# GpSimd subtracts half of the low parts for the first group of a DeltaNet layer

## The chip, the cores and the metric

The kernel runs on one core of a Trainium2 chip. A core has five engines with queues of their own: TensorE (PE in the rows; PEld is its weight load), VectorE (DVE), ScalarE (ACT), GpSimd (POOL) and SyncE (SP), which here issues the DMAs. The metric is the device time of one execution in microseconds; lower is better.

## The reference, cut to what matters

Two decoder layers on 512 tokens of width 1024 in float32. The first layer mixes tokens with a gated DeltaNet (8 heads of 128) beside 4 memory cross-attention heads; the second uses forgetting attention. The part that matters is the DeltaNet's input side:

```python
proj = h @ w_in
qkv = silu(causal_depthwise_conv(proj[..., :3 * MIX_WIDTH], conv_w))
z = proj[..., 3 * MIX_WIDTH: 4 * MIX_WIDTH]
q = l2_norm(split_heads(qkv[..., :MIX_WIDTH])) * HEAD_DIM ** -0.5
k = l2_norm(split_heads(qkv[..., MIX_WIDTH: 2 * MIX_WIDTH]))
v = split_heads(qkv[..., 2 * MIX_WIDTH:])
...
t_mat = triangular_solve(eye + a_mat, eye)      # per head and chunk
...
o = rms_norm(o, o_norm_w) * silu(split_heads(z))
```

## The kernel before, in words

Every projection is a product of float32 matrices, done in three matmuls (`mm3`, lines 157 to 159): each operand is split into a high part, which is a rounded copy, and a low part, which is the operand less that copy. For weights the split is made in `prepare`. Weights come in slabs of 128 partitions by 2048 columns, in two halves of 1024. For each half ScalarE makes the high part (L298) and then one engine subtracts (L299):

```python
for i in range(2):
    hi = self.wh.tile([P, 1024], F32R, ...)
    lo = self.wl.tile([P, 1024], F32R, ...)
    eng = nc.gpsimd if i and self.help else nc.vector
    ...
        nc.scalar.activation(hi[:, c], raw[i][:, c], AF.Copy)
        eng.tensor_sub(lo[:, c], raw[i][:, c], hi[:, c].bitcast(F32))
```

So with `self.help` set, the second half of a slab is subtracted by GpSimd, otherwise both halves by VectorE. In the kernel before, the flag is set for a while in the opening stage (the memory's keys and values) and is off from there on.

`slab` hands out the next slab that is ready and then calls `prepare(1)`, so that the slab after it is split while the present one is multiplied. The pools hold three raw tiles (`wr`), four high and four low halves, that is, two slabs. `fetch` issues the raw loads from SyncE; the order of all slabs is one list (`plan_weights`).

In `layer0_mixer` the keys come first, in four slabs of 256 columns (`gemm_feat`). Then the heads are done in two groups of four (`for g in range(2)`): two slabs of values, two of queries, both by `gemm_feat` with a convolution (`conv`: L727 on ScalarE, three steps L730 on VectorE that read PSUM, SiLU L732), and two of the gate z (`gemm_tok`, L1057). A slab is 48 matmuls of 512 columns.

Between these matmuls other work is interleaved. It is written as generators, which `pump` advances by a planned time after each `mm3`, so the order on TensorE is settled when the program is built; the order on the other engines follows from the dependences and a scheduler, and each engine runs its own queue in order. In the stretch of group 0 the interleaved work is: `dn_A` and `dn_inverse` of the DeltaNet (31 steps of two VectorE instructions each, L807 and L809, both inputs in SBUF; then two transposes L812, L813), and the four memory heads (`mem_heads`, `mem_attn`): cutting the queries (L451, L452), scores, maximum L639, exponential L642, reciprocal L643, normalization on GpSimd L644, transposes on TensorE, split L654 and L655. `group_scale` before them uses GpSimd at L429 and L435; the rsqrt by Newton steps is L207 to L211 on VectorE.

Of the kernel before, what the change touches and what calls it, by code (L numbers as in the profile page):

```python
# [41 lines left out]
class Kern:  # L42
# [962 lines left out]
    def layer0_mixer(self, hT):  # L1005
        nc, a = self.nc, self.a
        ab = self.const([P, NT, 16], "ab")
        qraw = self.slot(HD)
        qv = qraw.rearrange("p (t h) d -> p t (h d)", t=NT)

        def e0(t, ps):
            nc.scalar.copy(ab[:, t, :], ps[:, 0:16])
            nc.scalar.copy(qv[:, t, 0:256], ps[:, 16:272])

        def e1(t, ps):
            nc.scalar.copy(qv[:, t, 256:512], ps)

        self.gemm_tok(hT, e0, N=272, by_tile=True, need=lambda t: f"hx{t}")
        self.A = [self.slot(P) for _ in range(2)]
        self.spawn("dn", self.dn_gates(ab))  # L1020
        self.spawn("dn", self.dn_decays())
        self.gemm_tok(hT, e1, N=256)
        self.drain("rm")
        self.kT = [self.slot(T) for _ in range(2)]
        self.Ac = self.slot(1024)

        def ek(h, ps):
            self.conv(8 + h, ps, self.kT[h // 4][:, h % 4])
            self.spawn(f"dn{h % 2}", self.dn_A(h))

        for s in range(4):
            self.gemm_feat(hT, ek, 2 * s)
        self.spawn("mem", self.mem_heads(0, qraw))
        left = list(range(H))

        def merges():
            while "inverse" not in self.marks:
                yield 0.0
            while left:
                h = left.pop(0)  # L1040
                yield from self.dn_merge(h)
                self.free += 3
                self.marks.add(f"inv{h}")

        self.spawn("dn", self.dn_inverse())
        for i in range(3):
            self.spawn(f"dn{i}", merges())
        self.v, self.qT, self.z, self.mix = [None] * 2, [None] * 2, [None] * 2, [None] * 2
        for g in range(2):
            def ev(h, ps):  # L1050
                self.spawn("v", self.dn_v(h, self.conv(16 + h, ps)))

            def eq(h, ps):
                self.conv(h, ps, self.qT[g][:, h % 4])

            def ez(t, ps):
                nc.scalar.activation(self.z[g][:, t, :], ps, AF.Silu)  # L1057

            self.v[g] = self.slot(P)
            for s in range(2):  # L1060
                self.gemm_feat(hT, ev, 4 * g + 2 * s)
            self.qT[g] = self.slot(T)
            for s in range(2):
                self.gemm_feat(hT, eq, 4 * g + 2 * s)
            self.z[g] = self.slot(512)
            self.gemm_tok(hT, ez)
            self.drain("v")
            self.spawn("rec", self.dn_group(g))
# [463 lines left out]
```

## Time and profile before

| | us |
|---|---|
| median of 3 runs (lowest, highest) | 1437.98 (1436.66, 1438.18) |
| profiled execution, its own time | 1438.26 |
| its span, first to last instruction | 1436.6 |
| TensorE busy in the span | 1408.9 |
| VectorE busy in the span | 979.1 |
| ScalarE busy in the span | 688.4 |
| GpSimd busy in the span | 237.8 |

The times are of whole executions; the span leaves out what lies around the first and last instruction. Busy times are sums over the whole span; a stage can look quite different from the mean.

### The profile page before, as it was taken

The numbers are of one execution on the slowest core, as the hardware profiler recorded it, in microseconds if no ns is written. First come the engines' busy times: TensorE is split into PE (matmuls) and PEld (weight loads), VectorE is DVE, ScalarE is ACT, GpSimd is POOL, SyncE is SP. The second block draws the span as 40 slices with busy tenths as digits, with TensorE's granted clock in tenths as the row PEclk, the third lists the DMA queues.
The fourth block names the chain that finished last, engine by engine and source line by source line (L and its number), as shares of the span: only waits on it lengthen the run. The fifth ranks groups of instructions, "written<-read, shape, count | busy, mean of one in ns | idle before, by whom it ended". The sixth has DMA issues, their size and how long they took to land.

```text
span 1436.6 us, 19839 instructions
## 1 busy us (share of the span) xinstructions
PE 1408.9 (98%) x7442; PEld 1184.2 (82%) x7442; DVE 979.1 (68%) x1857; ACT 688.4 (48%) x1209; POOL 237.8 (17%) x321
## 2 busy tenths in 40 slices
PE   8999999989999999999999999999899999999999
PEld 6988777878889888888889888888788888888887
DVE  6679988477675677587657655665767567768663
ACT  6554764655344545444324454554534454554430
POOL 2274323222000000000001433533320000000000
PEclk9999999999999999999999999999999999999999
DMA  7542232134243151321226222224224315142122
GB/s 255 168 154 74 66 103 68 60 89 147 60 176 112 51 176 59 117 88 60 80 84 203 87 92 89 81 89 169 66 95 147 113 36 183 50 143 80 42 88 73
DMA packets 49634, 149.84 MB, mean 104 GB/s; under 512 B 5570, under 2 KB 10242, under 8 KB 49284
## 3 DMA queue, kind: packets, MB, share of 16 engines
q1 hardware_dynamic: 49392, 148.54, 31.6%
q8 instruction: 58, 0.95, 0.3%
q14 instruction: 36, 0.29, 0.1%
q10 hardware_dynamic: 148, 0.06, 0.0%
HBM read 141.20 MB, written 7.37 MB: 103 GB/s over the span
## 4 chain that ended last, share of the span: by engine, by line
PE 84%; DVE 10%; ACT 2%; issue 2%; DMA 1%; POOL 1%; SPq 0%; POOLq 0%; ACTq 0%; DVEq 0%
PE acc L157 20%; PE acc L158 19%; PE acc L159 19%; PE aux L159 6%; PE aux L157 6%; PE aux L158 6%; PE aux L164 3%; PE aux L169 3%; DVE wl L299 2%; DVE cv L730 1%; DVE slot L809 1%; DVE slot L807 1%; DVE cv L411 1%; DVE slot L1264 1%; ACT wh L298 0%
## 5 line engine op out<-in xcount | busy, mean ns | idle before, releaser
L157 PE MATMUL acc<-slot,wh 128*128 128x512 f32 (+1 forms) x832 | 314.3, 378 | 0.0
L299 DVE TENSOR_TENSOR wl<-wr,wh 128x1024 fp32r<-128x1024 f32 (+3 forms) x192 | 231.7, 1211 | 120.6 <-ACT wh L298 110.8
L158 PE MATMUL acc<-slot,wh 128*128 128x512 f32 (+1 forms) x832 | 310.9, 374 | 0.1
L159 PE MATMUL acc<-slot,wl 128*128 128x512 f32 (+1 forms) x832 | 310.8, 374 | 0.0
L298 ACT ACTIVATE wh<-wr 128x1024 fp32r<-128x1024 f32 (+3 forms) x194 | 197.0, 1016 | 199.4 <-PE acc L159 95.8
L157 PE MATMUL acc<-wh,slot 128*128 128x512 f32 (+3 forms) x740 | 285.0, 385 | 6.2 <-ACT wh L298 6.2
L158 PE MATMUL acc<-wl,slot 128*128 128x512 f32 (+3 forms) x740 | 276.8, 374 | 0.0
L159 PE MATMUL acc<-wh,slot 128*128 128x512 f32 (+3 forms) x740 | 276.3, 374 | 0.0
L159 PEld LDWEIGHTS acc<-slot,wl 128*128 128x128 f32 x832 | 156.7, 188 | 27.7
L157 PEld LDWEIGHTS acc<-slot,wh 128*128 128x128 f32 x832 | 156.7, 188 | 26.4
L158 PEld LDWEIGHTS acc<-slot,wh 128*128 128x128 f32 x832 | 156.9, 189 | 26.0 <-DVE slot L420 0.3
L157 PEld LDWEIGHTS acc<-wh,slot 128*128 128x128 f32 x740 | 140.7, 190 | 27.7 <-ACT wh L298 6.2
L1296 DVE TENSOR_TENSOR wl<-slot,wh 128x1024 fp32r<-128x1024 f32 x84 | 101.3, 1222 | 89.8 <-ACT wh L1295 89.8
L159 PEld LDWEIGHTS acc<-wh,slot 128*128 128x128 f32 x740 | 140.1, 189 | 24.7 <-DVE slot L1166 0.2
L158 PEld LDWEIGHTS acc<-wl,slot 128*128 128x128 f32 x740 | 140.7, 190 | 20.3 <-DVE wl L299 0.4
L1295 ACT CAST wh<-slot 128x1024 fp32r<-128x1024 f32 x84 | 88.3, 1052 | 92.8 <-PE acc L158 46.3
L157 PE MATMUL aux<-wh,t 128*128 128x512 f32 x336 | 130.8, 389 | 0.0
L159 PE MATMUL aux<-wh,t 128*128 128x512 f32 x336 | 130.7, 389 | 0.0
L158 PE MATMUL aux<-wl,t 128*128 128x512 f32 x336 | 130.7, 389 | 0.0
L429 POOL TENSOR_TENSOR cv<-slot 128x512 f32<-128x512 f32 x26 | 31.3, 1217 | 463.9 <-ACT slot L1189 421.0
L1264 DVE TENSOR_TENSOR slot<-slot,acc 128x512 f32<-128x512 f32 (+1 forms) x81 | 54.7, 677 | 51.4 <-PE acc L159 51.3
L1384 ACT ACTIVATE cv<-acc 128x512 f32<-128x512 f32 x64 | 37.6, 594 | 107.0 <-PE acc L159 107.0
(262 smaller groups left out, 1944.0 us busy)
## 6 DMA issues: line engine op xcount, KB each, us to landing
wr<-in_w_mlp SPq DMA_DIRECT2D x80, 512.0 KB, 4.3
slot<-in_w_mlp SPq DMA_DIRECT2D x48, 512.0 KB, 8.0
wr<-in_w_out SPq DMA_DIRECT2D x24, 512.0 KB, 3.8
wr<-in_fox_kq SPq DMA_DIRECT2D x16, 512.0 KB, 3.8
slot<-in_x SPq DMA_DIRECT2D x8, 512.0 KB, 6.6
wr<-in_dn_k SPq DMA_DIRECT2D x8, 512.0 KB, 4.3
wr<-in_dn_v SPq DMA_DIRECT2D x8, 512.0 KB, 3.7
wr<-in_dn_q SPq DMA_DIRECT2D x8, 512.0 KB, 3.8
```

Of the source, the lines that this page charges most:

```text
L157: mm(out, l[0], r[0], start=start, stop=False, **kw)
L158: mm(out, l[0], r[1], start=False, stop=False, **kw)
L159: mm(out, l[1], r[0], start=False, stop=stop, **kw)
L164: self.nc.tensor.matmul(out, l, r, start=start, stop=stop)
L169: self.nc.tensor.transpose(out, in_, self.ident)
L298: nc.scalar.activation(hi[:, c], raw[i][:, c], AF.Copy)
L299: eng.tensor_sub(lo[:, c], raw[i][:, c], hi[:, c].bitcast(F32))
L429: nc.gpsimd.tensor_mul(sq, raw[:, i:i + 4, :], raw[:, i:i + 4, :])
L1264: self.nc.vector.tensor_add(xv, xv, ps)
L1295: nc.scalar.copy(hi, r)
L1296: nc.vector.tensor_sub(lo, r, hi.bitcast(F32))
L1384: nc.scalar.activation(r, ps, AF.Relu)
```

## The change

One line sets the flag at the start of each group: on for group 0, off for group 1. `prepare` then gives the subtraction of each slab's second half to GpSimd for the slabs that are split while the flag is on.

```diff
@@ -1056,6 +1056,7 @@
             def ez(t, ps):
                 nc.scalar.activation(self.z[g][:, t, :], ps, AF.Silu)
 
+            self.help = g == 0
             self.v[g] = self.slot(P)
             for s in range(2):
                 self.gemm_feat(hT, ev, 4 * g + 2 * s)
```

## Rows read from the trace of the kernel before

**Rows 1.** The page: busy us of an engine, share of the span, instructions.

```profile
PE 1408.9 (98%) x7442; PEld 1184.2 (82%) x7442; DVE 979.1 (68%) x1857; ACT 688.4 (48%) x1209; POOL 237.8 (17%) x321
```

**Rows 2.** Busy times by window: stretch, length, busy us (instructions) by engine.

```profile
core 0: us, PE busy (x) PEld busy (x) DVE busy (x) ACT busy (x) POOL busy (x), PEclk, DMA share, GB/s
...
140.00:207.00 67.00, 61.87 (x304) 49.06 (x302) 65.40 (x124) 45.96 (x83) 17.47 (x18) 1.00 0.30 91
207.00:260.00 53.00, 50.15 (x561) 39.11 (x562) 36.20 (x69) 28.43 (x60) 22.65 (x29) 1.00 0.23 71
```

**Rows 3.** The chain of waits from 110 to 215 us: start, us, what.

```profile
164.25 4.03 DVE cv L730 x6
...
174.49 1.11 POOL t L644
...
207.07 0.54 DVE t L452
```

**Rows 4.** TensorE's waits, 140 to 220 us: total us, times, longest.

```profile
PE aux L169 <- POOL t L644: 3.6, 5, 1.7
```

**Rows 5.** Line 299: VectorE's from 118 to 197 us, GpSimd's in the whole kernel.

```profile
L299 DVE TENSOR_TENSOR wl<-wr,wh x11: 1209/1215/1757, 118.3 to 195.8; 128x1024 fp32r<-128x1024 f32 x11
...
L299 POOL TENSOR_TENSOR wl<-wr,wh x2: 2356/2378/2401, 15.9 to 22.6; 128x1024 fp32r<-128x1024 f32 x2
```

**Rows 6.** Timeline of GpSimd and VectorE in the opening stage.

```profile
22.62 2.40 POOL L299 TENSOR_TENSOR wl<-wr,wh 128x1024 fp32r<-128x1024 f32 x1 [4.37 <-ACT wh L298]
...
22.73 2.31 DVE L211 SCALAR_TENSOR_TENSOR sm<-sm,sm 128x2 f32<-128x2 f32 x1
```

**Rows 7.** Timeline of GpSimd and VectorE at 118 and at 173 us.

```profile
118.51 1.89 POOL L429 TENSOR_TENSOR cv<-slot 128x512 f32<-128x512 f32 x1 [3.14 <-ACT slot L732]
...
119.42 0.74 DVE L730 SCALAR_TENSOR_TENSOR cv<-acc,par,cv 128x509 f32<-128x509 f32 x1
...
172.85 1.11 POOL L644 TENSOR_TENSOR t<-t,sm 128x512 f32<-128x512 f32 x1 [4.88 <-DVE sm L643]
...
173.09 1.14 DVE L809 TENSOR_TENSOR slot<-slot 128x252 f32<-128x252 f32 x1
```

**Rows 8.** Timeline: six casts, the VectorE instructions behind them, L644, the first gate matmul.

```profile
114.65 1.05 ACT L298 ACTIVATE wh<-wr 128x1024 fp32r<-128x1024 f32 x1
...
127.19 1.06 ACT L298 ACTIVATE wh<-wr 128x1024 fp32r<-128x1024 f32 x1 [4.38 <-PE acc L158]
...
128.26 0.16 DVE L210 SCALAR_TENSOR_TENSOR sm<-sm,sm 128x16 f32<-128x16 f32 x1
...
143.14 1.06 ACT L298 ACTIVATE wh<-wr 128x1024 fp32r<-128x1024 f32 x1
...
144.62 0.17 DVE L209 TENSOR_TENSOR sm<-sm 128x32 f32<-128x32 f32 x1
...
155.27 1.06 ACT L298 ACTIVATE wh<-wr 128x1024 fp32r<-128x1024 f32 x1 [0.80 <-PE acc L158]
...
156.23 1.07 POOL L644 TENSOR_TENSOR t<-t,sm 128x512 f32<-128x512 f32 x1 [2.94 <-DVE sm L643]
...
156.44 1.02 DVE L809 TENSOR_TENSOR slot<-slot 128x135 f32<-128x135 f32 x1
...
174.20 0.48 PE L157 MATMUL acc<-wh,slot 128*128 128x512 f32 x1
...
176.60 1.07 ACT L298 ACTIVATE wh<-wr 128x1024 fp32r<-128x1024 f32 x1
...
178.38 0.41 DVE L807 TENSOR_TENSOR slot<-slot,slot 128x255 f32<-128x255 f32 x1
...
193.15 1.06 ACT L298 ACTIVATE wh<-wr 128x1024 fp32r<-128x1024 f32 x1
...
194.44 0.36 DVE L809 TENSOR_TENSOR slot<-slot 128x192 f32<-128x192 f32 x1
```

## The prediction

> **What bounds the kernel now.** The page comes first: TensorE is busy for 1408.9 of 1436.6 us, VectorE for 979.1 us [rows 1]. Read as a mean over the kernel, this says that VectorE's time is free. The change touches one stage only, so the busy times by window come next. They say the opposite there: between 140 and 207 us VectorE is busy for 65.40 of 67 us, while TensorE has 67.00 - 61.87 = 5.13 us of idle time at a granted clock of 1.00, its 2.4 GHz level; from 207 to 260 us VectorE is busy for only 36.20 of 53 us [rows 2]. So for about 67 us VectorE sets the pace and TensorE, which runs a fixed order of projection matmuls with pieces of memory attention between them, stops now and then for what VectorE hands over late.
>
> The chain of waits shows the same. In this stretch it runs along VectorE: 4.03 us of convolution at 164.25, through a GpSimd multiply at 174.49 to TensorE, and again along VectorE to L452 at 207.07, behind which TensorE goes on [rows 3]. TensorE's own waits name the place where lateness reaches it: five waits, 3.6 us in all, for GpSimd's L644, which normalizes the softmax with a reciprocal that VectorE makes [rows 4]. From this I take two things: what VectorE gains or loses before 207 us reaches the end nearly one for one, and a gain can be no larger than TensorE's idle 5.13 us plus a little of the next window.
>
> **What is moved.** `slab` splits one slab ahead. When the flag is set, the first slab of values is already split, and the last split before the flag falls is the first slab of the second group. So six slabs are affected (second values slab, both of queries, both of the gate, first values slab of group 1), with one second half each: six 128x1024 subtractions. Nothing else is added: the same casts on ScalarE, the same DMAs, the same matmuls.
>
> *Saved on VectorE.* One such subtraction takes 1.215 us, and there are eleven of them between 118.3 and 195.8 us; six of these go [rows 5]. Started one behind the other they cost less than that: the one at 118.3 is followed by a convolution step at 119.42 [rows 5, 7], 1.13 us later. Saved: 6 x 1.13 = 6.8 us.
>
> *Added on GpSimd.* The form is in the trace: two of them, 2356 and 2401 ns [rows 5]. Six give 6 x 2.38 = 14.3 us, and GpSimd is busy for only 17.47 of the 67 us [rows 2], so the engine has room.
>
> *What the added work does to VectorE.* In the opening stage such a GpSimd subtraction runs from 22.62 to 25.02. VectorE starts L211 at 22.73, on 128x2 elements that lie in SBUF with both inputs, and needs 2.31 us for it: it ends at 25.04, with the GpSimd instruction [rows 6]. The stage in question shows the same on a smaller scale: L809 on 252 elements takes 1.14 us at 173.09, beside a GpSimd multiply that runs from 172.85 to 173.96 [rows 7], against 0.41 us for L807 on 255 elements at 178.38 [rows 8]. It goes the other way too: GpSimd's L429 takes 1.89 us at 118.51, beside VectorE's subtraction at 118.3, where L644 of the same size takes 1.07 us at 156.23 [rows 5, 7, 8]. And it does not hit everything: the convolution step at 119.42, which reads PSUM and one tile of SBUF, takes its 0.74 us in the middle of that L429 [rows 7]. So a GpSimd subtraction of 2.38 us stops VectorE from its next instruction with both inputs in SBUF until it ends.
>
> The Trainium skill states this as a rule ("SBUF — State Buffer", section "Who interferes with whom"): a VectorE instruction with two SBUF inputs contends with a GpSimd instruction that reads SBUF, and whichever is second waits for the whole of the first. The traced 2.31 us for two elements per partition agrees. By engine durations alone, without that rule, the change would be a gain of up to 5.13 us; by the rule it is the sum that follows.
>
> *The sum.* GpSimd can begin when the cast of the same half ends. Casts end at 115.70, 128.25, 144.20, 156.33, 177.67 and 194.21; the next VectorE instruction with both inputs in SBUF starts at 118.3 (the subtraction that leaves), 128.26, 144.62, 156.44, 178.38 and 194.44 [rows 5, 8]. With 2.36 us from each cast's end, VectorE loses 0, 2.35, 1.94, 2.25, 1.65 and 2.13 us: 10.3 us in all. Net: 10.3 - 6.8 = 3.5 us later at 207 us. VectorE has 67.00 - 65.40 = 1.60 us of idle time in the stretch [rows 2] that can take up a part; I take 0.3 of it. That leaves 3.2 us, and L452, at which TensorE already waits, passes all of it on. After 207 us VectorE has idle time, but TensorE (50.15 of 53 us busy) has not, and it is TensorE that is late.
>
> The positions are uncertain, since the order on each engine is settled for the new program as a whole. Bounds for one subtraction: VectorE loses nothing if it meets a run of convolution steps (4.03 us long at 164.25 [rows 3]), and 2.36 us at most. Six times that, less 6.8 us, spans -6.8 to +7.4 us, the first cut by TensorE's idle time to about -5.1.
>
> *What is hidden.* The weights are not late: z's second half would be split at 156.33 + 2.36 = 158.7, and the first gate matmul starts at 174.20 [rows 8], a cover of over 15 us; the other five are split just as far ahead, one slab of 48 matmuls before their use. The raw tiles come free earlier for the halves that VectorE now reaches late, so SyncE's next loads are issued earlier; nothing in the waits of TensorE names a load here, so this is worth nothing. On GpSimd, behind each subtraction stand the multiplies of the memory heads and of the values; the ones that matter are those of L644.
>
> **Rivals.** *Faster.* The subtractions fall beside VectorE instructions that read PSUM (convolution steps, L655, L639), and each costs VectorE 0.6 us or less: 6.8 - 3.6 = 3.2 us gained, of TensorE's 5.13 us idle: 1438.3 - 3.2 = 1435.1 in the profiled run's terms. It decides when the six together cost less than 6.8 - 2.9 = 3.9 us. For it: the first one, which costs nothing. Against: all five later places cost 1.65 to 2.35 us.
>
> *No change.* Losses and savings cancel at 1.13 us lost per subtraction: the order would have to put about half of them beside convolutions. 1437 to 1440.
>
> *Slower through GpSimd's queue.* The fourth subtraction is ready at 156.33 and L644 starts at 156.23 [rows 8]. Should L644 stand behind it, it begins at 158.7, and TensorE, which waits for it at that moment, stands 2.4 us longer; another L644 follows the cast that ends at 194.21. Since VectorE is late by then anyway, the two overlap, and I give it 1 to 2.5 us each: 1443 to 1446. For it: the readiness within 0.1 us. Against: L644 belongs to an earlier piece of the program.
>
> **How the numbers follow.** The profiled execution took 1438.26 us around its span of 1436.6; the median is 1437.98, 0.28 less. With 3.2 us on 1438.26 that is 1441.5, and beside the median 1441.2 us. About 0.2% (2.9 us) is what a measurement can tell from no change: 1435.1 to 1440.9. Chances: forecast 0.45 (its own range 1439.5 to 1443), no change 0.28, faster 0.17, queue 0.10. The forecast lies just beyond the bound, so about a fifth of it counts as no change: slower 0.45, same 0.38, faster 0.17. The range leaves out the far ends of faster and queue: 1435 to 1445.5.
>
> **What would show it.** Six rows of L299 on GpSimd, some 2.4 us each, between 115 and 200 us. Beside each but the first, one VectorE instruction (L209 to L211, L807, L809, L299) that takes 1.5 to 2.5 us in place of 0.2 to 0.4. VectorE still over 97% busy from 140 to about 210 us, L452 some 3 us later than 207, and TensorE's idle time in the stretch up from 5.1 to about 8 us. It would be wrong if the six cost VectorE under 4 us, if TensorE had slack at L452 that the waits don't show, or if the order of the memory heads against the projections changes so that other waits replace these.

## The result and the profile after

| | before | after |
|---|---|---|
| median of 5 runs, us | 1437.58 | 1450.57 |
| ratio, 95% interval | | 1.0086 [1.0074, 1.0098] |
| span of the profiled execution, us | 1436.6 | 1448.8 |

The change costs 13.0 us. The forecast was 3.2 us, with 1445.5 us as the top of the range: the sign was right, the size four times too small, and the range missed. The medians leave out three slow executions: one of before beside the experiments (4069.79 us), one of old_order_first_three (1557.83) and one of old_order_moved (1750.78), which was the traced one.

The page first: its row of busy times and its row of the granted clock in 40 slices.

```profile
PE 1413.9 (98%) x7442; PEld 1188.9 (82%) x7442; DVE 980.4 (68%) x1851; ACT 691.2 (48%) x1211; POOL 251.0 (17%) x327
...
PEclk9999899999999999999999999999999999999999
```

Beside [rows 1], VectorE's busy time has gone up by 1.3 us although six subtractions have left it (x1857 to x1851), and GpSimd's by 13.2 us. The second row has one digit below 9, in the fifth slice, which is the stage in question (145 to 181 us). In the page of before all 40 digits are 9.

Busy times by window after, for the two windows of [rows 2].

```profile
140.00:207.00 67.00, 59.91 (x281) 48.68 (x282) 60.73 (x117) 40.31 (x74) 25.30 (x22) 0.92 0.21 65
207.00:260.00 53.00, 47.42 (x460) 37.23 (x459) 37.27 (x60) 30.43 (x57) 18.90 (x23) 0.94 0.23 71
```

The prediction wanted VectorE over 97% busy here. It is busy for 60.73 of 67 us (91%), less than before. TensorE stands still for 7.09 us (5.13 before), and its mean granted clock is 0.92, where it was 1.00.

TensorE's waits after, 110 to 260 us: total us, times, longest.

```profile
PE aux L169 <- POOL t L644: 4.9, 3, 3.1
PE aux L158 <- DVE t L655: 3.9, 1, 3.9
PE aux L169 <- ACT cv L732: 2.7, 1, 2.7
PE aux L158 <- POOL t L600: 1.8, 1, 1.8
```

Against [rows 4]: L644 still leads, but as three waits with a longest of 3.1 us in place of five with a longest of 1.7, and three other waits stand beside it (the rows leave out two smaller ones). L452, on which the prediction let its whole sum pass, is not among them.

The subtractions after, GpSimd's and VectorE's of the stage (groups by line).

```profile
L299 POOL TENSOR_TENSOR wl<-wr,wh 128x1024 fp32r<-128x1024 f32 x6 | 14.4, 2401 | 10.8 <-ACT wh L298 10.8
L299 DVE TENSOR_TENSOR wl<-wr,wh 128x1024 fp32r<-128x1024 f32 x9 | 11.3, 1254 | 4.5 <-issue 3.0 <-ACT wh L298 1.5
```

Six on GpSimd at 2.4 us, as [rows 5] let expect. What stands beside them on VectorE is in the timeline of both engines after.

```profile
129.43 2.40 POOL L299 TENSOR_TENSOR wl<-wr,wh 128x1024 fp32r<-128x1024 f32 x1
...
129.50 2.36 DVE L211 SCALAR_TENSOR_TENSOR sm<-sm,sm 128x16 f32<-128x16 f32 x1
...
147.77 2.39 POOL L299 TENSOR_TENSOR wl<-wr,wh 128x1024 fp32r<-128x1024 f32 x1 [0.34 <-ACT wh L298]
148.28 1.93 DVE L211 SCALAR_TENSOR_TENSOR sm<-sm,sm 128x32 f32<-128x32 f32 x1
...
170.35 2.71 DVE L730 SCALAR_TENSOR_TENSOR cv<-acc,par,cv 128x510 f32<-128x510 f32 x4
170.52 2.39 POOL L299 TENSOR_TENSOR wl<-wr,wh 128x1024 fp32r<-128x1024 f32 x1 [5.87 <-ACT wh L298]
...
203.10 2.42 POOL L299 TENSOR_TENSOR wl<-wr,wh 128x1024 fp32r<-128x1024 f32 x1
203.31 2.35 DVE L809 TENSOR_TENSOR slot<-slot 128x112 f32<-128x112 f32 x1
```

Three VectorE instructions are held up, as in [rows 6]: 2.36, 1.93 and 2.35 us, each to the end of its GpSimd neighbour. The other three subtractions, among them the one at 170.52, lie beside steps that read PSUM (L730, L655), and these take 0.68 to 0.75 us each, as without a neighbour. Unblocked, the three take 0.17, 0.18 and 0.28 us (new_order_busy_no_read, below), so VectorE lost 2.19 + 1.75 + 2.07 = 6.0 us and saved 6.8. By the prediction's sum that is no loss at all. Yet 13 us are gone.

The chain of waits after, 125 to 215 us, runs over all three, and between them over the GpSimd subtraction at 170.52 and the L600 that stands behind it in GpSimd's queue.

```profile
129.58 2.28 DVE sm L211
...
148.36 1.84 DVE sm L211
...
158.91 1.13 POOL t L644
160.08 0.69 PE aux L169 x2
...
170.52 2.39 POOL wl L299
172.90 0.69 POOL t L600
...
203.31 2.36 DVE slot L809
...
211.62 0.79 PE aux L158
```

At TensorE's longer stops lie three stretches in which the trace records half the granted clock, the 1.2 GHz level: from 142.04 for 3.41 us, from 159.11 for 6.83 and from 210.31 for 6.83, 17.1 us in all. TensorE had stood still for 2.69, 3.06 and 3.85 us, up to 140.64, 160.08 and 211.62; the first stretch begins 1.4 us behind its stop, the other two about 1 us before the end of theirs. The insides of the three by window:

```profile
142.10:145.40 3.30, 3.30 (x9) 2.54 (x8) 3.30 (x6) 1.46 (x3) 0.00 (x0) 0.50 0.00 0
159.20:165.80 6.60, 5.72 (x19) 4.86 (x20) 6.08 (x10) 1.76 (x3) 1.87 (x2) 0.50 0.25 79
210.40:217.00 6.60, 5.38 (x15) 4.31 (x16) 2.88 (x4) 1.30 (x3) 0.00 (x0) 0.50 0.33 112
```

TensorE is busy for 14.40 of these 16.50 us, at half speed. Scaled to 17.1 us that is 14.9 us of busy time at half speed, or some 7.4 us lost, an estimate. The window from 105 to 330 us, first before, then after:

```profile
105.00:330.00 225.00, 213.15 (x1484) 174.34 (x1483) 183.22 (x423) 131.12 (x273) 74.18 (x93) 1.00 0.27 81
```

```profile
105.00:330.00 225.00, 206.88 (x1407) 169.03 (x1405) 175.90 (x384) 124.63 (x255) 87.59 (x99) 0.96 0.24 73
```

Idle time of TensorE: 225.00 - 213.15 = 11.85 before, 18.12 after. These windows hold the same time, but not the same work. Over the same work, from the projection matmul that starts at 105.02 us in the trace of before to the one that starts there at 235.01, the stage takes 129.99 us before and 143.69 after. Of the 13.7 us, 7.2 are idle time of TensorE (7.49 to 14.72) and 6.5 are longer busy time for the same matmuls (122.50 to 128.97). So about half of the loss is stops and the other half is the half clock, a little less than the estimate. Behind the stage the distance stays at some 14 us up to 1000 us, and falls to 12.3 behind a stretch of 3.41 us at half clock at 1021.86 in the trace of before, which after doesn't have; the spans differ by 12.2 us.

One more thing changed that no line of the diff names. The order in which the engines issue the stage's instructions is made by the scheduler when the program is built, and it came out differently. Besides the six, 164 of 680 TensorE instructions of the stage, 161 of 384 of VectorE and 42 of 175 of ScalarE stand in other places of their queues, by the lists of both orders in the experiments' kernels. On TensorE it is the interleaved pieces that moved against the projections: 62 of their matmuls and transposes stand earlier, by up to 24 projection matmuls, and 9 later. The first place in the stage where the two TensorE lists differ (- before, + after; from the built programs, so with buffer numbers):

```
 L157 MATMUL acc_1495<-slot_216,wh_1297 128x512
+L169 MATMUL aux_1536<-ident,cv_1471 128x128 x4
+L169 MATMUL aux_1561<-ident,slot_460 128x128 x4
 L158 MATMUL acc_1495<-slot_218,wh_1297 128x512
...
 L159 MATMUL acc_1496<-slot_216,wl_1298 128x512
-L169 MATMUL aux_1536<-ident,cv_1471 128x128 x4
-L169 MATMUL aux_1561<-ident,slot_460 128x128 x4
```

The transposes of the first values stand five projection matmuls sooner, and in front of them lies the wait of 2.7 us for L732.

### The profile page after: what moved, and what is told of

The parts are those of the page before. It is cut to its first block, busy times and chain, and to the rows that moved or that the text cites. A ratio compares the mean times of both kernels' runs of the same rounds, so it can differ in the third digit from the quotient of the medians.

```text
span 1448.8 us, 19844 instructions
## 1 busy us (share of the span) xinstructions
PE 1413.9 (98%) x7442; PEld 1188.9 (82%) x7442; DVE 980.4 (68%) x1851; ACT 691.2 (48%) x1211; POOL 251.0 (17%) x327
## 4 chain that ended last, share of the span: by engine, by line
PE 86%; DVE 8%; ACT 2%; issue 2%; POOL 1%; DMA 1%; SPq 0%; ACTq 0%; POOLq 0%
PE acc L157 20%; PE acc L158 20%; PE acc L159 20%; PE aux L158 6%; PE aux L159 6%; PE aux L157 6%; PE aux L164 4%; PE aux L169 3%; DVE cv L730 1%; DVE slot L809 1%; DVE slot L807 1%; DVE sm L211 1%; DVE wl L299 1%; DVE cv L411 1%; DVE slot L1265 1%
## 5 line engine op out<-in xcount | busy, mean ns | idle before, releaser
L299 DVE TENSOR_TENSOR wl<-wr,wh 128x1024 fp32r<-128x1024 f32 (+3 forms) x186 | 223.8, 1207 | 120.9 <-ACT wh L298 110.3
```

## The experiments

Theory A: VectorE is blocked while GpSimd reads, and TensorE passes the loss on. Theory B: the new order of issue costs the time, whoever subtracts. Rival C: GpSimd's queue, since L600 and L644 stand behind the subtractions. (The expectations call A the port theory and B the order theory.) Rival D: half clock on TensorE costs time of its own. In the labels "old order" is the order of before and "new order" that of after, written out for some 1350 instructions of the stage, and "moved" means that GpSimd subtracts.

All results together. Idle is TensorE's from 105 to 330 us (225.00 less its busy time by window), half clock the time at 0.50 in the same stretch by the trace's record of the clock, and in brackets what of it lies before 235 us. Stage is how much longer than before the traced execution takes from the projection matmul that starts at 105.02 us in the trace of before to the one that starts there at 235.01, and in brackets what of it is idle time of TensorE. Differences in the text are of medians, against 1437.58 us; the runs of before beside the other kernels had medians of 1436.84 to 1437.67 us.

| run | median us | ratio to before, 95% interval | idle us | half clock us (before 235) | stage us (idle) |
|---|---|---|---|---|---|
| before | 1437.58 | | 11.85 | 0 | 0 |
| after | 1450.57 | 1.0086 [1.0074, 1.0098] | 18.12 | 17.1 (17.1) | +13.7 (7.2) |
| old_order_moved | 1444.49 | 1.0050 [1.0036, 1.0063] | | | |
| old_order_moved_again | 1444.97 | 1.0053 [1.0040, 1.0067] | 17.08 | 6.8 (3.4) | +7.4 (5.8) |
| new_order_not_moved | 1446.07 | 1.0059 [1.0045, 1.0073] | 17.29 | 10.2 (10.2) | +9.7 (5.4) |
| old_order_no_read | 1437.37 | 0.9999 [0.9990, 1.0008] | 10.48 | 3.4 (0) | -2.5 (-2.0) |
| new_order_no_read | 1438.96 | 1.0007 [0.9998, 1.0016] | 11.90 | 3.4 (0) | +0.4 (0.7) |
| old_order_busy_no_read | 1436.60 | 0.9991 [0.9982, 1.0000] | 9.85 | 3.4 (0) | -1.9 (-1.4) |
| new_order_busy_no_read | 1437.86 | 0.9999 [0.9990, 1.0007] | 11.12 | 6.8 (3.4) | +1.4 (0.2) |
| old_order_first_one | 1437.40 | 0.9998 [0.9989, 1.0007] | 11.36 | 3.4 (0) | +0.1 (0.1) |
| old_order_first_three | 1440.32 | 1.0021 [1.0012, 1.0030] | 14.45 | 0 | +2.6 (2.4) |
| old_order_last_three | 1441.40 | 1.0033 [1.0021, 1.0046] | 14.91 | 3.4 (0) | +3.6 (3.6) |
| old_order_done_twice | 1446.47 | 1.0063 [1.0048, 1.0077] | 17.99 | 10.2 (6.8) | +9.6 (6.6) |
| old_order_four_pieces | 1440.15 | 1.0017 [1.0007, 1.0026] | 12.65 | 3.4 (0) | +1.5 (1.5) |
| new_order_four_pieces | 1445.50 | 1.0057 [1.0045, 1.0069] | 15.95 | 6.8 (6.8) | +6.3 (3.6) |
| changed_stops_filled | 1446.07 | 1.0059 [1.0047, 1.0072] | 10.78 | 3.4 (0) | +7.4 (-1.7) |

The half clock behind 235 us says nothing of the move: all fifteen traces, that of before too, have a stop of 2.6 to 2.9 us that ends between 303 and 321 us, and in ten of them a stretch of 3.41 us at half clock lies at it, with the move and without.

**The order and the move apart.** The order is fixed by an ordering dependence without a semaphore between neighbours of one engine; the moved six are left out of the lists. No run fixes an order without another change; nearest is old_order_first_one, which stands at 0.9998 of before.

```diff
+def pin(tc):
+    ins = {i.name: i for i in tc.nc.cur_bb.bb.instructions}
+    for row in ORDER:
+        for a, b in zip(row, row[1:]):
+            tc.add_manual_dep(ins[f"I-{b}"], f"I-{a}",
+                              mybir.DependencyInfo(mybir.DependencyClass.NoSync, mybir.DependencyReason.DATA),
+                              reason="issue order")
...
     Kern(ctx, tc, a).run()
+    pin(tc)
```

old_order_moved is the changed kernel with the lists of before, new_order_not_moved the kernel before with the lists of after.

> The six subtractions on GpSimd as in the changed kernel, but every other instruction on every engine issued in the order of the kernel before. Port theory (GpSimd's subtractions block VectorE through the shared SBUF port, and that is the loss): still slower than before, by the 3 us of the prediction or more, up to 13. Order theory (moving six instructions made the scheduler issue all engines' work in another order, and that order is the loss): within 3 us of before, 1435 to 1441, with no new half-speed stretch of the clock.

> The six subtractions back on VectorE, but every other instruction issued in the order of the changed kernel. Port theory: as before, 1435 to 1441, since nothing new runs on GpSimd. Order theory: nearly all of the loss stays, 1446 to 1453, with stops of TensorE near 138, 157 and 208 us and half-speed clock behind them.

Each alone costs about 8 us: 6.9 and 7.4 for the move in the old order (the kernel was run twice), 8.5 for the new order with the subtractions on VectorE. Neither A nor B alone is the cause, and the two don't add up to 16 but to 13. The trace read here is that of old_order_moved_again.

> The same kernel as old_order_moved (six subtractions on GpSimd, every other instruction of the stage in the order of before), once more for its trace. If GpSimd's reading is what holds VectorE up, five of the six subtractions stand beside a VectorE instruction with both inputs in SBUF that takes 1.5 to 2.4 us, TensorE's stops between 140 and 235 us add up to 5 us more than before, and 1445 us comes out. If VectorE is not held up more than in the changed kernel (three instructions, some 6 us against 6.8 us saved), the 8 us must come from stops of TensorE behind GpSimd's own work (L600, L644) and from stretches at half clock.

Timeline of GpSimd and VectorE in old_order_moved_again, at the second to the sixth subtraction:

```profile
128.31 2.39 POOL L299 TENSOR_TENSOR wl<-wr,wh 128x1024 fp32r<-128x1024 f32 x1
...
128.38 2.35 DVE L210 SCALAR_TENSOR_TENSOR sm<-sm,sm 128x16 f32<-128x16 f32 x1
...
149.52 2.41 POOL L299 TENSOR_TENSOR wl<-wr,wh 128x1024 fp32r<-128x1024 f32 x1
149.53 3.48 DVE L299 TENSOR_TENSOR wl<-wr,wh 128x1024 fp32r<-128x1024 f32 x1
...
160.14 2.46 POOL L299 TENSOR_TENSOR wl<-wr,wh 128x1024 fp32r<-128x1024 f32 x1
160.39 2.39 DVE L809 TENSOR_TENSOR slot<-slot 128x156 f32<-128x156 f32 x1
...
181.82 2.38 POOL L299 TENSOR_TENSOR wl<-wr,wh 128x1024 fp32r<-128x1024 f32 x1 [2.15 <-ACT wh L298]
...
182.46 2.03 DVE L807 TENSOR_TENSOR slot<-slot,slot 128x255 f32<-128x255 f32 x1
...
201.37 2.48 POOL L299 TENSOR_TENSOR wl<-wr,wh 128x1024 fp32r<-128x1024 f32 x1
201.64 2.42 DVE L809 TENSOR_TENSOR slot<-slot 128x175 f32<-128x175 f32 x1
```

These are five blocked instructions, each ending with its GpSimd neighbour, but for L299, which then takes its own time as well. The same instructions in old_order_busy_no_read (below), where nothing blocks them, take 0.17, 1.21, 0.32, 0.41 and 0.34 us. Lost: 2.18 + 2.27 + 2.07 + 1.62 + 2.08 = 10.2 us, where the prediction had summed 10.3. So in the order for which it was made, the sum on VectorE holds, net 10.2 - 6.8 = 3.4 us. What doesn't hold is that TensorE loses only the net: its idle time went up by 5.2 us, with a stretch of 3.41 us at half clock in the stage on top, and the median by 7.4 us.

**Which of the six.** In the old order, only some of them moved.

```diff
-            self.help = g == 0
+            self.help = [1, 1, 1, 0, 0, 0] if g == 0 else []
...
-                eng = nc.gpsimd if i and self.help else nc.vector
+                eng = nc.gpsimd if i and self.help and (self.help is True or self.help.pop(0)) else nc.vector
```

old_order_last_three has the list [0, 0, 0, 1, 1, 1], old_order_first_one [1, 0, 0, 0, 0, 0].

> Order of before; only the first subtraction (second values slab, at 116 us) on GpSimd: the one that meets convolution steps, which read PSUM, and for which the prediction took a loss of 0 and a gain of 1.13 us. If VectorE sets the pace from there to 207 us: 1436 us, 1.1 faster. If VectorE's lateness at 116 us does not reach TensorE: within 0.5 us of before.

> Order of before; only the first three subtractions (second values slab, both queries slabs) on GpSimd. If each subtraction has its own price on VectorE: by the terms of the prediction 0 + 2.35 + 1.94 - 3 x 1.13 = +0.9 us, about 1438. If the loss of 8 us sits in the stops around 140 to 160 us, +4 to +8 us here and nearly none with the last three alone.

> Order of before; only the last three (both gate slabs, first values slab of group 1) on GpSimd. By the terms of the prediction 2.25 + 1.65 + 2.13 - 3 x 1.13 = +2.6 us, about 1440. If the loss sits in GpSimd's queue before L644 and in front of L452 at 207 us, +4 to +8 us. If the two halves add up, this and old_order_first_three together make the 8 us of all six; if a stop of TensorE past some length costs extra through half clock, each alone is cheaper than half of it.

The first one, which meets steps that read PSUM, frees VectorE of 1.13 us at no loss, and gains nothing that can be measured. The others cost 2.7 us (first three) and 3.8 us (last three); 6.6 us together, near the 7.4 of all six. There is no single bad place. By the netted terms it should have been 0.9 and 2.6. The stage came out at 2.6 and 3.6 us, between these and the gross losses on VectorE: two blocked instructions (4.4 us) and three (5.7 us).

**What GpSimd does in that time.** In place of a subtraction GpSimd sets the low half to zero (the low parts of six halves are left out). VectorE is freed, and GpSimd reads nothing. One memset takes 0.95 us; in the "busy" kernels two and a half of them keep GpSimd as long as a subtraction did.

```diff
-                    eng.tensor_sub(lo[:, c], raw[i][:, c], hi[:, c].bitcast(F32))
+                    if eng is nc.gpsimd and self.mine:
+                        eng.memset(lo[:, c].bitcast(F32), 0.0)
+                        eng.memset(lo[:, c].bitcast(F32), 0.0)
+                        eng.memset(lo[:, :512].bitcast(F32), 0.0)
+                    else:
+                        eng.tensor_sub(lo[:, c], raw[i][:, c], hi[:, c].bitcast(F32))
```

> Order of the kernel before; GpSimd fills the six low halves with zeros in place of the subtraction, so VectorE is rid of six subtractions and nothing that reads SBUF is added on GpSimd (the low parts of six weight halves are left out). Port theory: the 6.8 us freed on VectorE come through as far as TensorE's idle time allows, 3 to 5 us faster than before (1433 to 1435). Order theory says the same here, for it has the same order; if it is no faster, VectorE's pace was not what bounded the stretch.

> Order of the changed kernel; GpSimd fills the six low halves with zeros in place of the subtraction (their low parts are left out). Port theory: the loss goes, 1433 to 1440. Order theory: the loss stays but for what VectorE's three blocked instructions took (2.36, 1.93 and 2.35 us), 1443 to 1451.

> Order of before; in place of each of the six subtractions GpSimd sets the low half to 0 two and a half times (three memsets, about 2.4 us together, nothing read; the low parts of six halves are left out). VectorE is freed of the six, GpSimd's queue is as long occupied as by the subtractions. If GpSimd's reading costs the 7 us (VectorE blocked), this stays where one memset each left it, at 1437.4. If the queue costs them (L600 and L644 stand behind the work), it comes to 1441 to 1445.

> The same two and a half memsets in the order of the changed kernel (low parts of six halves left out). One memset each gave 1439.0, the subtractions 1450.6. If reading makes the difference: about 1439. If the time that GpSimd is taken from L600 and L644 makes it: 1445 to 1450.

All four stand within about 0.1% of before. Rival C falls: GpSimd may be taken from L600 and L644 for 2.4 us six times, in either order, and the medians show no loss; against one memset each, the stage is 0.6 and 1.0 us longer. The same place as above, in old_order_busy_no_read (here L814 is L809 of before):

```profile
157.62 0.95 POOL L300 MEMSET wl<- 128x1024 f32 x1
157.89 0.32 DVE L814 TENSOR_TENSOR slot<-slot 128x156 f32<-128x156 f32 x1
```

The instruction that took 2.39 us beside the subtraction takes 0.32 us beside the memset. It is the reading that blocks. The Trainium skill ("SBUF — State Buffer", section "Who interferes with whom") says as much: a VectorE instruction with two SBUF inputs contends with a GpSimd instruction that reads SBUF, not with one that only writes it. The two durations agree.

The four also say what the relief is worth. In the old order VectorE is freed of 6.8 us and the median gains 0.2 or 1.0 us, the stage 2.5 or 1.9; the expectation had asked for 3 to 5. In the new order, with the subtractions on VectorE, 1446.07 becomes 1437.86 without them: the same 6.8 us are worth 8.2, with 6.8 us less at half clock in the stage. So what a relief is worth depends on the order. The new order is not bad in itself: it calls the pieces on TensorE earlier, costs next to nothing when VectorE is free of the six and not blocked, and 8 us when VectorE is not.

**Loss without relief.** In the old order VectorE keeps all subtractions, and GpSimd does the six once more behind it, into the same tile.

```diff
-                    eng.tensor_sub(lo[:, c], raw[i][:, c], hi[:, c].bitcast(F32))
+                    if eng is nc.gpsimd and self.mine:
+                        nc.vector.tensor_sub(lo[:, c], raw[i][:, c], hi[:, c].bitcast(F32))
+                        eng.tensor_sub(lo[:, c], raw[i][:, c], hi[:, c].bitcast(F32))
+                    else:
+                        eng.tensor_sub(lo[:, c], raw[i][:, c], hi[:, c].bitcast(F32))
```

> Order of before; VectorE keeps all its subtractions and GpSimd does the six once more behind them, into the same tile. VectorE has the losses without the relief of 6.8 us. If gain and loss on VectorE are netted, as the prediction did it, this is 6.8 us later than old_order_moved: about 1451 to 1452. If the relief is worth nothing to TensorE and only the losses reach it, it is as slow as old_order_moved: 1444 to 1446.

At 1446.47 us it is 1.5 us slower than old_order_moved_again, not 6.8. Its five blocked instructions lost 9.5 us, and its stage is 9.6 us longer than before (6.6 of it stops, 3.0 busy time at half clock), 2.2 more than that of old_order_moved_again. So in this order TensorE sees the losses, half clock included, about one for one, and of the relief some 2 of 6.8 us, as in the kernels with memsets. One of the five has a single input in SBUF (timeline of old_order_done_twice):

```profile
139.38 2.41 POOL L301 TENSOR_TENSOR wl<-wr,wh 128x1024 fp32r<-128x1024 f32 x1 [1.37 <-PE aux L169]
139.70 2.12 DVE L207 TENSOR_SCALAR sm<-ssk 128x32 int32<-128x32 int32 x1
```

Unblocked, this L207 takes 0.17 us (old_order_busy_no_read).

**Shorter GpSimd instructions.** Each of the six cut into four of 128x256, in either order.

```diff
+                    if eng is nc.gpsimd and self.mine:
+                        for k in range(4):
+                            d = slice(256 * k, 256 * k + 256)
+                            eng.tensor_sub(lo[:, d], raw[i][:, d], hi[:, d].bitcast(F32))
+                    else:
+                        eng.tensor_sub(lo[:, c], raw[i][:, c], hi[:, c].bitcast(F32))
```

> Order of before; each of the six subtractions on GpSimd cut into four of 128x256. If a VectorE instruction waits for one GpSimd instruction and not for GpSimd's whole queue, the five VectorE instructions that took 2.0 to 2.4 us, or 2.3 us longer than alone, wait at most some 0.6 us each time, and the two engines take turns: 1438 to 1442. If each VectorE instruction behind it is blocked anew, or GpSimd keeps the port from piece to piece, it stays at 1445.

> The changed kernel in its own order; each of the six subtractions on GpSimd cut into four of 128x256. In the order of before this cost 2.5 us where the uncut subtractions cost 7.4. If blocked VectorE instructions are behind most of the 12 us by which the changed kernel is slower than the same order with nothing read: 1440 to 1444. If it is the sum of what GpSimd reads and not the length of one instruction: 1448 to 1451.

The two engines take turns, as this stretch of old_order_four_pieces shows (L812 is L807 of before):

```profile
159.05 3.23 POOL L302 TENSOR_TENSOR wl<-wr,wh 128x256 fp32r<-128x256 f32 x4
159.30 0.74 DVE L814 TENSOR_TENSOR slot<-slot 128x156 f32<-128x156 f32 x1
160.08 0.76 DVE L812 TENSOR_TENSOR slot<-slot,slot 128x175 f32<-128x175 f32 x1
```

VectorE waits some 0.4 us at a time, GpSimd needs 3.23 us instead of 2.46, and VectorE's instructions lose 5.5 us in all instead of 10.1 (durations from 105 to 235 us compared one by one with old_order_busy_no_read). The cost falls from 7.4 to 2.6 us in the old order and from 13.0 to 7.9 us in the new one, where VectorE's loss is 3.1 us instead of 6.1. The first answers the expectation by theory A; the second goes the same way but stays above its 1440 to 1444. Why does the new order turn less loss on VectorE into more on TensorE? Set against the busy kernel of the same order, over the same work, after has 7.1 us more stops for the 6.1 that VectorE lost, and new_order_four_pieces 3.4 for 3.1; old_order_moved_again has 7.1 more for 10.1, and old_order_four_pieces 2.9 for 5.5. So in the new order the loss reaches the stops whole, in the old one in part, and after pays 5.2 us for the half clock on top where old_order_moved_again pays 2.2. That pieces called earlier forgive less lateness would fit, but no run shows it by itself.

**Half clock.** The changed kernel in its own order, with TensorE kept busy ahead of its five longest stops by 84 matmuls of 128x128 that multiply by zero.

```diff
+    def fill(self, out, start, l=None):
+        name = out.tensor.name.rsplit("_", 1)[0]
+        for _ in range(FILL.pop((name, start), 0)):
+            self.nc.tensor.matmul(out[:, :P], self.zero if l is None else l, self.zero, start=start, stop=start)
...
         mm(out, l[0], r[0], start=start, stop=False, **kw)
+        self.fill(out, False, l[0])
...
     def tr(self, out, in_):
+        self.fill(out, True)
```

> The changed kernel in its own order, with 84 more matmuls on TensorE: in front of the five longest stops of the stage (18, 22, 10, 6 and 28 of 128x128, which multiply by zero), so that TensorE is busy in most of the time in which it would wait. They do no work that is needed. If the stretches at half clock behind these stops cost time of their own (17.1 us at half clock, about 7 us of work lost): the granted clock stays at 1.00 from 140 to 235 us, and 1443 to 1445 us comes out. If VectorE's lateness sets the pace whatever TensorE does, the clock stays up and the stops only get longer: 1449 to 1451.

The window from 105 to 330 us in changed_stops_filled, and two later ones:

```profile
105.00:330.00 225.00, 214.22 (x1511) 177.73 (x1510) 176.40 (x392) 125.33 (x256) 86.69 (x98) 0.99 0.23 73
300.00:330.00 30.00, 25.53 (x168) 22.95 (x168) 21.64 (x61) 11.33 (x43) 9.63 (x8) 0.94 0.26 79
1010.00:1050.00 40.00, 36.09 (x168) 29.81 (x168) 27.85 (x55) 20.45 (x33) 17.61 (x26) 0.91 0.24 83
```

More matmuls, none of them needed, make the kernel 4.5 us faster (1450.57 to 1446.07; 1.0086 to 1.0059 of the runs of before beside each). Between 105 and 300 us no stretch at half clock is left. So half clock costs time of its own, and rival D holds. The stage gained more than the median: the projection matmul that starts at 236.00 us after starts at 228.85 here, 7.2 us earlier, of which 0.9 were there before 105 us. In this trace two stretches at half clock lie at 315 and 1029 us (3.41 and 6.83 us, the two lower rows), and the profile of after has none there. The 84 matmuls took 10.1 us on TensorE; over the same work its idle time shrank by 8.9 (14.72 to 5.81). The stops didn't get longer, as they would if VectorE set the pace whatever TensorE does. What is left, 7.4 us in the stage, is what the move alone costs in the old order. The expectation of 1443 to 1445 was a little too good.

No kernel came out clearly faster than before. The best that computes everything, old_order_first_one, is level with it.

## Why the prediction was wrong, by its own steps

- *VectorE sets the pace from 140 to 207 us.* Right as a reading of [rows 2], but the weaker half of the truth. With 6.8 us of VectorE's work gone and the order kept, TensorE's idle time falls by 2.0 us (11.85 to 9.85) and the median by 1.0 us at most. VectorE is busy nearly throughout, and yet most of what was taken from it is not what TensorE waits for.
- *What is moved and saved.* Six subtractions at 2.40 us each, as said; 6.8 us saved on VectorE.
- *Each blocks VectorE.* The mechanism was right, and so, in the order of before, was the price: 10.2 us measured against 10.3, on L210, L299, L809, L807 and L809. In the changed kernel three of the six fell beside steps that read PSUM, and the loss was some 6 us.
- *"What VectorE gains or loses before 207 us reaches the end nearly one for one."* This is the step that failed, for what VectorE gains. Losses and gains were netted, 10.3 - 6.8, before they were passed on. In the order of before, which the sum took, the losses passed about one for one, half clock included: 9.5 us on VectorE made the stage 9.6 us longer in old_order_done_twice. Of the relief of 6.8 us only 1.9 to 2.5 reached TensorE (the memset kernels), and old_order_first_one gained nothing from a free 1.13 us. So the net of 3.4 us became 7.4 us. In the new order the relief is worth more, 8.2 us, but TensorE begins 8.5 us behind.
- *No term for TensorE's clock.* The sum took a longer stop at its length. [rows 2] show 1.00 throughout, and the prediction carried that over to the kernel after. In the kernel after, 17.1 us at half clock made TensorE's busy time 6.5 us longer over the same work, and filling the stops brought 4.5 us back in the median, 6.3 in the stage.
- *The order of the others stays.* The prediction named a change of order as what would make it wrong, and gave it no chance and no price. TensorE, VectorE and ScalarE were ordered anew. In the new order the six subtractions cost 12.7 us against the same order with nothing read (1437.86), where in the old one they cost 8.4 (against 1436.60), although VectorE lost less (6.1 against 10.1): its losses reached TensorE's stops whole, and more half clock stood behind them.
- *Rivals.* Faster: half of the subtractions did land beside steps that read PSUM, as this rival wanted, and it was slower still. The queue before L644: the two "busy" runs exclude it, alone, as the cause of more than about 1 us.

How the 13.0 us split between blocking and order can't be said as a sum: either alone costs about 8 us, and without GpSimd's reading the new order costs nothing that can be measured (0.9999). What stays open is why the half-clock stretches come where they do. The stop of 2.57 us in the trace of before, up to 306.78, has none behind it, and ten other traces have one at the same stop; in new_order_busy_no_read a stop of 1.95 us, up to 198.09, has one.

## What to carry to other kernels

Don't net gains against losses on an engine that others wait for: here the losses came through about whole, and of the gains less than a half as long as the order stayed. Where TensorE's idle time is split into short stops, price a longer stop with the work that is done at half clock behind it. Before a streaming operation goes to GpSimd, list the VectorE instructions that will stand beside it; if it must go, cut it into short pieces, and compare the order of issue of the two programs before believing any sum.

## What the runs showed that was not expected

- VectorE's L207, which has one input in SBUF (int32, 128x32), was held for 2.12 us beside GpSimd's subtraction; unblocked it takes 0.17 us. The prediction had counted only instructions with two. The Trainium skill ("SBUF — State Buffer", section "Who interferes with whom") names tensor_scalar, which L207 is, among the operations that can take the port pair shared with GpSimd, in its two-port modes; the row agrees with the first, and doesn't show the mode.
- Needless matmuls in front of stops made the changed kernel 4.5 us faster, since they kept the granted clock at 1.00 in the stage.
- The two engines take turns: four GpSimd pieces took 3.23 us beside VectorE where one subtraction took 2.46, and nearly halved what VectorE lost.
